# Making a modulation vector in 48 parts beside the first layer's attention instead of beside its gated heads

## The chip, the cores and the metric

The kernel runs on one core of a Trainium2 chip. The metric is device microseconds of one execution. A core has TensorE (PE in the profile, its weight loads are PEld), VectorE (DVE), ScalarE (ACT), GpSimd (POOL) and SyncE (SP), each with an instruction queue of its own that is worked off in order, and 16 DMA engines that are fed from the queues of SP and, for some loads, of POOL.

## The reference

Two blocks are computed in float32 on a sequence of 1024 tokens of width 1024. The first block has two layers. Layer 0 projects its input to eight heads of banded attention (three dilations, 1, 4 and 16) and to four heads of a gated scan in both directions; their outputs are gated and projected back (`w_out_ab`), and a layer norm follows. Layer 1 has twelve gated-scan heads. The second block is a modulated mixer (pooling, state-space and delta-rule branches) and a mixture of 16 experts.

What the change touches is one small piece of the second block, which depends on nothing that the first computes:

```python
sc = jax.nn.silu(c)
scc = jax.nn.silu(c_ctx)[None]
m_lat = jnp.split(sc @ ada_w[l] + ada_b[l], 6, axis=-1)
m_ctx = jnp.split(scc @ ada_w[l] + ada_b[l], 6, axis=-1)
h_lat = modulate(rms_norm(x, norm1_g[l]), m_lat[0], m_lat[1])
h_ctx = modulate(rms_norm(ctx, norm1_g[l]), m_ctx[0], m_ctx[1])
```

`ada_w` is 1024 x 6144. All 6144 columns are wanted for `sc`, and the first 2048 for `scc`.

## The kernel before, in words

The program is written in tile form: Python code issues instructions in program order, and a scheduler then orders each engine's queue from a plan of its own, in which what stands earlier in the program goes first and later work fills in where an engine is free (a block marked `high_priority` goes ahead of its place). The order of each queue is fixed when the program is built; at run time an engine waits at the head of its queue until what the instruction needs is there.

The order of the program is: `Layer0` is set up; `l0.heads(range(4), early)` runs the four gated heads of layer 0 (`Gated`), each with its projections (matmuls into the PSUM tag `mm`, three for each product, since every operand is split in a high and a low part `whi`/`wlo`, `xh`/`xl`); after head 3, `early` adds the first two input projections of the attention (`l0.inputs`) and, in the kernel before, `modulation()`. Then `l0.attention` runs four pairs of attention heads (`attention_pair`). For each pair there are three dilations `p`, two halves and two steps `tp`, so 4 x 3 x 2 x 2 = 48 steps. A step makes scores on PE (`a`), soft maxes them on DVE and ACT (`p`, `pe`), transposes them on PE through the two one-buffer PSUM tags `tr` and `f`, used in turn by `bank()`, copies them out (`pT`) and multiplies by the values into `o`. `filler` adds the input projections of the later pairs, and the output projection (`OutProj`, matmuls `mm<-whi,yin`) follows in the program and fills in. Its `yin` loads are issued from POOL's queue.

`ada` makes the modulation vector `mods` in 48 blocks of 128 columns. For each block it loads two halves of the weight (`aw`, 128 x 4 x 128, two buffers), multiplies each of the eight 128 x 128 slices by a column of `silu(c)` and adds them up in `aacc`. This is done for the latent vector (v = 0) in all blocks and for the context vector (v = 1) in blocks 0 to 15. A sum is made either on DVE (eight instructions, L961 and L963, each a multiply and add) or on POOL (eight multiplies L966, two double-width adds L967, three adds L969 and L972, in place in `aw`). A matmul with a column of ones (L978) then sums over the partitions into the PSUM tag `f`, DVE adds the bias row `ar` (L979), and the row goes to `mods` in memory (L980). The first readers of `mods` are the rows `msh` and `msc` of the context inputs, which come after the output projection of layer 0. In the kernel before, v = 1 is made on DVE, and v = 0 on DVE in 16 of the 48 blocks (`j % 3 == 2`).

L116 makes `wlo` on POOL. In `Gated.unit`, L187 to L210 are DVE work, L239 and L241 POOL work, L214 and L249 PE work; L288 and L289 (`s_rs`) on POOL come ahead of `s_y` on DVE and the transposes L314. L533 to L537 close an attention pair on DVE.

Of the kernel before, what the change touches and what calls it, by code (L numbers as in the profile page):

```python
# [27 lines left out]
def dap(ap, dims, off=0):  # L28

    return bass.AP(tensor=ap.tensor, offset=ap.offset + off, ap=[list(d) for d in dims])  # L30
# [292 lines left out]
    nc.sync.dma_start(ydram[chunk].rearrange("i p t -> p i t")[:, :, t0:t0 + n], hl.bitcast(F32))  # L323


def attention_pair(g, pool, ydram, pair, qT, qp, kT, gate, vd, bias, spread, before):

# [49 lines left out]
    for p, half in ((0, 0), (0, 1), (1, 0), (1, 1), (2, 0), (2, 1)):  # L379
        o = g.psum("o")  # L380
        if half == 0:
# [4 lines left out]
            if p == 2:  # L386
                v16 = pool.tile([64, 16, P], F32, name="v16", tag="v16", bufs=1)
                nc.sync.dma_start(v16, dap(vd, [[16 * W, 64], [W, 16], [1, P]], f0))
        for tp in range(2):

            Ss = [g.psum("a") for _ in range(2)]
            pts = [pool.tile([P, 512], F32, name="pT", tag="pT", bufs=4) for _ in range(2)]
# [202 lines left out]
def bias_tiles(g, pool, rd, pair):  # L595
    out = []
    for h in range(2):
        ts = []
        for p in range(3):
            n, w = (P, 256) if p < 2 else (64, 64)  # L600
            b = pool.tile([P, w], F32, name=f"bias{h}{p}", tag=f"bias{h}{p}", bufs=1)
            for e in range(P // n):
                g.nc.sync.dma_start(b[n * e:n * e + n],
                                    dap(rd, [[383, n], [1, w]], ((pair * 2 + h) * 3 + p) * P * 384 + 127 + (0 if p < 2 else 64)))
            ts.append(b)
        out.append(ts)
    return out
# [20 lines left out]
class Layer0:  # L628
# [130 lines left out]
                self.head(h, gp, qp)  # L759
                after(h)  # L760

    def attention(self, filler):
        g = self.g
        with g.pool("attn") as ap, g.pool("attn2") as qp:
            self.side, rest = ap, lambda: None
            spread = ap.tile([48, 8, P], F32R, name="spread")
            g.nc.vector.memset(spread.bitcast(F32), 0.0)
            for i in (0, 32):
                g.nc.vector.tensor_copy(spread[i:i + 16].rearrange("r j (h f) -> r j h f", h=2),
                                        g.ident[:16, :16].rearrange("r (h j) -> r j h", h=2)[:, :, :, None].to_broadcast([16, 8, 2, 64]))  # L770
            qp_ = ap.tile([P, T], F32, name="qp")
            for pair in range(4):
                ts = []
                for nm in "qkg":
                    ts.append(qp.tile([P, T], F32, name=nm, tag=nm, bufs=1 + (nm != "g")))
                    g.nc.sync.dma_start(ts[-1], self.store[nm, pair])
                rest = attention_pair(g, ap, self.ydram, pair, ts[0], qp_, *ts[1:], self.vd, bias_tiles(g, ap, self.bd, pair), spread, rest)
                if pair == 3:
                    rest()
                filler(pair)  # L780


class OutProj:
# [155 lines left out]
def ada(g, pool, out):  # L939

    nc, I = g.nc, g.I
    c = pool.tile([P, 2, 8], F32, name="ac")
    sg = pool.tile([P, 2, 8], F32, name="acs")
    nc.sync.dma_start(c, I["c2"])
    sigmoid(g, sg, c)
    nc.vector.tensor_mul(c, c, sg)
    ones = pool.tile([P, 1], F32, name="aones")
    nc.vector.memset(ones, 1.0)
    n = 128
    for j in range(6144 // n):  # L950
        both = j < 2048 // n
        acc = [pool.tile([P, n], F32, name=f"aacc{v}", tag=f"aacc{v}", bufs=1) for v in range(1 + both)]
        for kh in range(2):
            w = pool.tile([P, 4, n], F32, name="aw", tag="aw", bufs=2)
            nc.sync.dma_start(w, I["ada_w"][:, 4 * kh:4 * kh + 4, j * n:(j + 1) * n])
            for v in ((1, 0) if both else (0,)):
                at = lambda k: c[:, v, 4 * kh + k:4 * kh + k + 1]
                if v == 1 or j % 3 == 2:
                    for k in range(4):
                        if kh + k == 0:  # L960
                            nc.vector.tensor_scalar(acc[v], w[:, k], at(k), None, op0=ALU.mult)  # L961
                        else:
                            nc.vector.scalar_tensor_tensor(acc[v], w[:, k], at(k), acc[v], op0=ALU.mult, op1=ALU.add)  # L963
                    continue
                for k in range(4):
                    nc.gpsimd.tensor_scalar(w[:, k], w[:, k], at(k), 0.0, op0=ALU.mult, op1=ALU.add)  # L966
                nc.gpsimd.tensor_add(w[:, 0:2], w[:, 0:2], w[:, 2:4])  # L967
                if kh == 0:
                    nc.gpsimd.tensor_add(acc[v], w[:, 0], w[:, 1])  # L969
                else:  # L970
                    for k in range(2):
                        nc.gpsimd.tensor_add(acc[v], acc[v], w[:, k])  # L972
        for v in range(1 + both):
            r = pool.tile([1, n], F32, name="ar", tag="ar", bufs=1)
            nc.sync.dma_start(r, dap(I["ada_b"], [[0, 1], [1, n]], j * n))
            ps = g.psum("tr")
            with g.tc.high_priority():
                nc.tensor.matmul(ps[:1, :n], ones, acc[v], start=True, stop=True)  # L978
                nc.vector.tensor_add(r, ps[:1, :n], r)  # L979
            nc.sync.dma_start(dap(out, [[0, 1], [1, n]], v * 6144 + j * n), r)  # L980


def rms_rstd(g, pool, xt, n=D, eps=EPS2, junk=None):
# [1265 lines left out]
def body(g, out):  # L2249
# [28 lines left out]
    pe = ExitStack()  # L2278
    pe.enter_context(g.psum_pool("ps1", mm=2, a=2, o=2, tr=1, f=1))
    g.open_w()  # L2280
    def modulation():
        g.aside = "f"
        with g.pool("ada") as ap:
            ada(g, ap, mods)
        g.aside = None
    x0s, l0s, es = ExitStack(), ExitStack(), ExitStack()
    xp = x0s.enter_context(g.pool("x0", "right"))
    l0 = Layer0(g, l0s, load_xT(g, xp, I["xT"]), yd)
# [1 line left out]
    def early(h):  # L2290
        if h == 3:
            l0.inputs(0)
            l0.inputs(1)
            modulation()
    l0.heads(range(4), early)
    ga = gains("gla_gain", 8)
    with es:
        def filler(pair):
            if pair < 2:
                l0.inputs(2 + pair)  # L2300
        l0s.close()
        l0.attention(filler)
        x0s.close()
        out0 = OutProj(g, es, "z0", "right", I["x"], yd, I["w_out0"],
                       lambda c: None if c < 4 else ga[:, c - 4:c - 3])
        for cs in ((4, 5), (6, 7), (8, 9), (1, 2), (10, 11, 0)):
            out0.group(*cs)
        x1s = ExitStack()
        xp = x1s.enter_context(g.pool("x1"))
        xt = [xp.tile([P, 8, T], F32R, name=n) for n in ("x1h", "x1l")]  # L2310
        g.aside = "f"
        with g.pool("cm") as mp:
            cx = context_inputs(g, mp, mods)
        g.aside = None
        states = (g.dram.tile([2, P, 384], F32, name="sstates"), g.dram.tile([3, 2, P, 64], F32, name="gstates"))
        rest = context_path(g, cx, states, "left")

        def aside(parts):
            g.aside = "f"
            for _ in range(parts):  # L2320
                next(rest, None)
            g.aside = None
        aside(4)
        closing(0, out0, "right", x1d, (3,), (), lambda zp, zt, tok: to_feature_major(g, zt, tok, xt))
# [152 lines left out]
```

## Time and profile before

| what | value |
|---|---|
| median of 3 runs | 3604.42 us (3601.4 to 3604.8) |
| the profiled execution | 3603.5 us, span 3601.4 us |
| PE busy | 3217.0 us (89% of the span) |
| DVE busy | 2527.6 us (70%) |
| ACT busy | 1577.9 us (44%) |
| POOL busy | 1383.2 us (38%) |

"Busy" is a sum over the whole span; it says nothing of a stage. A busy PE is not a PE at its peak, since matmuls overlap and their ends are modelled. The granted clock of PE is given as a share of 2.4 GHz; its two levels are 2.4 and 1.2 GHz.

### The profile page before, as it was taken

Reading aid. Unit: us, or ns where it says so; the run is one execution under the profiler, and the core shown is the slowest. Engines: PE = TensorE matmul, PEld = TensorE weight load, DVE = VectorE, ACT = ScalarE, POOL = GpSimd, SP = SyncE. Lnnn points to the kernel's source line nnn. Section 1 sums busy time; section 2 is a strip of 40 time slices with the busy share of each in tenths; the row PEclk is TensorE's granted clock in tenths of the full one; section 3 lists DMA queues with packets and bytes.
Section 4 is the critical chain, followed back from the end, with each engine's and each line's share of the span. In section 5 each row is a group of like instructions: output and inputs, shape, how many; then the busy total and the mean of one; then the engine's idle time right before and its main releaser. Section 6 shows DMA issues by size and latency. Waiting matters only on the chain.

```text
span 3601.4 us, 63422 instructions
## 1 busy us (share of the span) xinstructions
PE 3217.0 (89%) x23688; PEld 2585.4 (72%) x23688; DVE 2527.6 (70%) x5574; ACT 1577.9 (44%) x3344; POOL 1383.2 (38%) x1415
## 2 busy tenths in 40 slices
PE   7998898999979999999999989869897777849997
PEld 6887786766658878788887877656676666637765
DVE  4777664346685686987668677758996665578876
ACT  3444333544424454545546452235342432126765
POOL 4657673000043233433324331443222564335533
PEclk9999999999999999999999999879998888969999
DMA  5233344252343222111112234234345755668994
GB/s 183 77 92 92 95 130 144 80 190 75 100 140 99 64 68 58 55 60 52 41 49 68 66 134 136 82 88 120 103 131 142 168 148 173 230 193 317 378 348 156
DMA packets 374000, 461.27 MB, mean 128 GB/s; under 512 B 150419, under 2 KB 280723, under 8 KB 373692
## 3 DMA queue, kind: packets, MB, share of 16 engines
q1 hardware_dynamic: 359852, 407.93, 36.3%
q0 software_dynamic: 13840, 49.29, 4.4%
q8 instruction: 187, 3.06, 0.4%
q14 instruction: 121, 0.99, 0.1%
HBM read 357.57 MB, written 104.27 MB: 128 GB/s over the span
## 4 chain that ended last, share of the span: by engine, by line
PE 49%; DVE 22%; DMA 9%; issue 8%; POOL 7%; ACT 3%; SPq 2%; DVEq 0%; POOLq 0%; ACTq 0%
PE mm L139 10%; PE mm L140 9%; PE mm L141 9%; POOL aw L966 2%; PE a L249 2%; DVE cacc L1145 2%; PE a L406 1%; PE a L2041 1%; DMA aw<-in_ada_w_dram 1%; DMA srow<-rdsl 1%; PE a L141 1%; PE a L140 1%; PE o L225 1%; PE a L139 1%; POOL wlo L116 1%
## 5 line engine op out<-in xcount | busy, mean ns | idle before, releaser
L116 POOL TENSOR_TENSOR wlo<-wraw,whi 128x1024 fp32r<-128x1024 f32 (+1 forms) x131 | 328.3, 2510 | 525.6 <-ACT whi L115 513.2
L139 PE MATMUL mm<-x1h,whi 128*128 128x512 f32 x576 | 234.9, 408 | 3.3 <-DVE G L921 1.7
L140 PE MATMUL mm<-x1l,whi 128*128 128x512 f32 x576 | 233.4, 405 | 1.7 <-DVE x1l L133 1.7
L141 PE MATMUL mm<-x1h,wlo 128*128 128x512 f32 x576 | 233.5, 405 | 0.0
L139 PE MATMUL mm<-whi,x1h 128*128 128x256 f32 x768 | 221.8, 289 | 0.4 <-DVE G L921 0.4
L141 PE MATMUL mm<-whi,x1l 128*128 128x256 f32 x768 | 219.6, 286 | 0.0
L140 PE MATMUL mm<-wlo,x1h 128*128 128x256 f32 x768 | 219.0, 286 | 0.0
L2029 DVE TENSOR_TENSOR elo<-eraw,ehi 128x1024 fp32r<-128x1024 f32 x136 | 184.8, 1381 | 47.1 <-ACT ehi L2027 46.7
L2027 ACT CAST ehi<-eraw 128x1024 fp32r<-128x1024 f32 x160 | 165.5, 1051 | 99.6 <-PE a L141 35.9
L115 ACT CAST whi<-wraw 128x1024 fp32r<-128x1024 f32 (+1 forms) x131 | 136.1, 1040 | 153.9 <-PE mm L140 76.2
L140 PE MATMUL mm<-wlo,xh 128*128 128x256 f32 x640 | 184.2, 288 | 1.9 <-POOL wlo L116 1.9
L141 PE MATMUL mm<-whi,xl 128*128 128x256 f32 x640 | 184.4, 289 | 0.0
L139 PE MATMUL mm<-whi,xh 128*128 128x256 f32 x640 | 183.6, 288 | 0.9 <-DVE G L623 0.9
L139 PE MATMUL mm<-x2h,whi 128*128 128x512 f32 x400 | 166.9, 417 | 10.2 <-ACT cu L1134 5.6
L139 PE MATMUL mm<-whi,yin 128*128 128x512 f32 x352 | 151.4, 433 | 25.0 <-DVE z L824 14.0
L141 PE MATMUL mm<-x2h,wlo 128*128 128x512 f32 x400 | 164.3, 412 | 0.8 <-POOL wlo L116 0.8
L140 PE MATMUL mm<-x2l,whi 128*128 128x512 f32 x400 | 164.6, 411 | 0.0
L139 PE MATMUL mm<-xh,whi 128*128 128x512 f32 x336 | 138.6, 412 | 20.4 <-ACT whi L115 17.6
L966 POOL TENSOR_SCALAR aw<-aw,ac 128x128 f32<-128x128 f32 x256 | 123.7, 498 | 85.7 <-DMA aw<-in_ada_w_dram 41.6
L139 PEld LDWEIGHTS mm<-whi,x1h 128*128 128x128 f32 x768 | 146.7, 191 | 3.1 <-issue 1.0
L140 PEld LDWEIGHTS mm<-wlo,x1h 128*128 128x128 f32 x768 | 146.7, 191 | 0.6
L141 PEld LDWEIGHTS mm<-whi,x1l 128*128 128x128 f32 x768 | 146.8, 191 | 0.3
(747 smaller groups left out, 10317.0 us busy)
## 6 DMA issues: line engine op xcount, KB each, us to landing
eraw<-in_we_gate_dram SPq DMA_DIRECT2D x64, 512.0 KB
eraw<-in_we_up_dram SPq DMA_DIRECT2D x64, 512.0 KB
eraw<-in_we_down_dram SPq DMA_DIRECT2D x64, 512.0 KB
yin<-yd POOLq DMA_DIRECT2D x29, 1024.0 KB, 9.6
aw<-in_ada_w_dram SPq DMA_DIRECT2D x96, 256.0 KB
yd<-y_hl SPq DMA_DIRECT2D x80, 256.0 KB
wraw<-in_w_dram SPq DMA_DIRECT2D x25, 512.0 KB
wraw<-in_w_out_dram SPq DMA_DIRECT2D x24, 512.0 KB
```

The source lines that it names most:

```text
L115: nc.scalar.copy(hi[:, :sz], raw[:, :sz])
L116: nc.gpsimd.tensor_tensor(lo[:, :sz], raw[:, :sz], hi[:, :sz].bitcast(F32), op=ALU.subtract)
L139: nc.tensor.matmul(ps, sh, mh, start=first and i == 0, stop=False)
L140: nc.tensor.matmul(ps, sh, ml, start=False, stop=False)
L141: nc.tensor.matmul(ps, sl, mh, start=False, stop=last and i == n - 1)
L225: nc.tensor.matmul(up[:, :Vd], kdT[:, i * P:(i + 1) * P], V[:, gi, :], start=True, stop=True)
L249: nc.tensor.matmul(ap[32 * c:32 * c + 32, o + lo:o + hi], sta[:, o + 32 * c:o + 32 * c + 32], mov[:, o + lo:o + hi], start=True, stop=True)
L406: nc.tensor.matmul(Ss[h][:, i * 256:i * 256 + w], q[hs[h], qc:qc + P], k[hs[h], lo:lo + w], start=True, stop=True)
L966: nc.gpsimd.tensor_scalar(w[:, k], w[:, k], at(k), 0.0, op0=ALU.mult, op1=ALU.add)
L1145: nc.vector.scalar_tensor_tensor(acc, u[:, i:i + n], cw[:, i:i + 1], acc, op0=ALU.mult, op1=ALU.add)
L2027: nc.scalar.copy(hi, raw)
L2029: nc.vector.tensor_sub(lo, raw, hi.bitcast(F32))
```

## The change

`ada` becomes a generator that yields after each block, and `modulation()` is gone. `attention_pair` draws the next block at the head of each of its 48 steps, so that each block stands in the program just ahead of a step; the tiles come from the pool `attn2` of the attention. The scratch row `aacc` of v = 0 has two buffers and not one. The work is shared out anew: v = 1 stays on DVE (blocks 0 to 15), v = 0 is made on DVE only in six blocks (`j % 6 == 5` from block 16 on: 17, 23, 29, 35, 41, 47) and on POOL in 42. The matmul and the bias add are no longer marked `high_priority`. The PSUM tag is `f` in both kernels (in the one before by `g.aside`).

```diff
--- before.py
+++ after.py
@@ -323,7 +323,7 @@
     nc.sync.dma_start(ydram[chunk].rearrange("i p t -> p i t")[:, :, t0:t0 + n], hl.bitcast(F32))
 
 
-def attention_pair(g, pool, ydram, pair, qT, qp, kT, gate, vd, bias, spread, before):
+def attention_pair(g, pool, ydram, pair, qT, qp, kT, gate, vd, bias, spread, before, aside):
 
 
 
@@ -387,6 +387,7 @@
                 v16 = pool.tile([64, 16, P], F32, name="v16", tag="v16", bufs=1)
                 nc.sync.dma_start(v16, dap(vd, [[16 * W, 64], [W, 16], [1, P]], f0))
         for tp in range(2):
+            next(aside, None)
 
             Ss = [g.psum("a") for _ in range(2)]
             pts = [pool.tile([P, 512], F32, name="pT", tag="pT", bufs=4) for _ in range(2)]
@@ -759,10 +760,11 @@
                 self.head(h, gp, qp)
                 after(h)
 
-    def attention(self, filler):
+    def attention(self, filler, aside):
         g = self.g
         with g.pool("attn") as ap, g.pool("attn2") as qp:
             self.side, rest = ap, lambda: None
+            aside = aside(qp)
             spread = ap.tile([48, 8, P], F32R, name="spread")
             g.nc.vector.memset(spread.bitcast(F32), 0.0)
             for i in (0, 32):
@@ -774,10 +776,12 @@
                 for nm in "qkg":
                     ts.append(qp.tile([P, T], F32, name=nm, tag=nm, bufs=1 + (nm != "g")))
                     g.nc.sync.dma_start(ts[-1], self.store[nm, pair])
-                rest = attention_pair(g, ap, self.ydram, pair, ts[0], qp_, *ts[1:], self.vd, bias_tiles(g, ap, self.bd, pair), spread, rest)
+                rest = attention_pair(g, ap, self.ydram, pair, ts[0], qp_, *ts[1:], self.vd, bias_tiles(g, ap, self.bd, pair), spread, rest, aside)
                 if pair == 3:
                     rest()
                 filler(pair)
+            for _ in aside:
+                pass
 
 
 class OutProj:
@@ -949,35 +953,38 @@
     n = 128
     for j in range(6144 // n):
         both = j < 2048 // n
-        acc = [pool.tile([P, n], F32, name=f"aacc{v}", tag=f"aacc{v}", bufs=1) for v in range(1 + both)]
+        acc = [pool.tile([P, n], F32, name=f"aacc{v}", tag=f"aacc{v}", bufs=2 - v) for v in range(1 + both)]
         for kh in range(2):
             w = pool.tile([P, 4, n], F32, name="aw", tag="aw", bufs=2)
             nc.sync.dma_start(w, I["ada_w"][:, 4 * kh:4 * kh + 4, j * n:(j + 1) * n])
-            for v in ((1, 0) if both else (0,)):
-                at = lambda k: c[:, v, 4 * kh + k:4 * kh + k + 1]
-                if v == 1 or j % 3 == 2:
-                    for k in range(4):
-                        if kh + k == 0:
-                            nc.vector.tensor_scalar(acc[v], w[:, k], at(k), None, op0=ALU.mult)
-                        else:
-                            nc.vector.scalar_tensor_tensor(acc[v], w[:, k], at(k), acc[v], op0=ALU.mult, op1=ALU.add)
-                    continue
+            at = lambda v, k: c[:, v, 4 * kh + k:4 * kh + k + 1]
+            on_dve = [1] if both else [0] if j % 6 == 5 else []
+            for v in on_dve:
+                a = acc[v]
                 for k in range(4):
-                    nc.gpsimd.tensor_scalar(w[:, k], w[:, k], at(k), 0.0, op0=ALU.mult, op1=ALU.add)
-                nc.gpsimd.tensor_add(w[:, 0:2], w[:, 0:2], w[:, 2:4])
-                if kh == 0:
-                    nc.gpsimd.tensor_add(acc[v], w[:, 0], w[:, 1])
-                else:
-                    for k in range(2):
-                        nc.gpsimd.tensor_add(acc[v], acc[v], w[:, k])
+                    if kh + k == 0:
+                        nc.vector.tensor_scalar(a, w[:, k], at(v, k), None, op0=ALU.mult)
+                    else:
+                        nc.vector.scalar_tensor_tensor(a, w[:, k], at(v, k), a, op0=ALU.mult, op1=ALU.add)
+            if 0 in on_dve:
+                continue
+            a = acc[0]
+            for k in range(4):
+                nc.gpsimd.tensor_scalar(w[:, k], w[:, k], at(0, k), 0.0, op0=ALU.mult, op1=ALU.add)
+            nc.gpsimd.tensor_add(w[:, 0:2], w[:, 0:2], w[:, 2:4])
+            if kh == 0:
+                nc.gpsimd.tensor_add(a, w[:, 0], w[:, 1])
+            else:
+                for k in range(2):
+                    nc.gpsimd.tensor_add(a, a, w[:, k])
         for v in range(1 + both):
             r = pool.tile([1, n], F32, name="ar", tag="ar", bufs=1)
             nc.sync.dma_start(r, dap(I["ada_b"], [[0, 1], [1, n]], j * n))
-            ps = g.psum("tr")
-            with g.tc.high_priority():
-                nc.tensor.matmul(ps[:1, :n], ones, acc[v], start=True, stop=True)
-                nc.vector.tensor_add(r, ps[:1, :n], r)
+            ps = g.psum("f")
+            nc.tensor.matmul(ps[:1, :n], ones, acc[v], start=True, stop=True)
+            nc.vector.tensor_add(r, ps[:1, :n], r)
             nc.sync.dma_start(dap(out, [[0, 1], [1, n]], v * 6144 + j * n), r)
+        yield
 
 
 def rms_rstd(g, pool, xt, n=D, eps=EPS2, junk=None):
@@ -2278,11 +2285,6 @@
     pe = ExitStack()
     pe.enter_context(g.psum_pool("ps1", mm=2, a=2, o=2, tr=1, f=1))
     g.open_w()
-    def modulation():
-        g.aside = "f"
-        with g.pool("ada") as ap:
-            ada(g, ap, mods)
-        g.aside = None
     x0s, l0s, es = ExitStack(), ExitStack(), ExitStack()
     xp = x0s.enter_context(g.pool("x0", "right"))
     l0 = Layer0(g, l0s, load_xT(g, xp, I["xT"]), yd)
@@ -2291,7 +2293,6 @@
         if h == 3:
             l0.inputs(0)
             l0.inputs(1)
-            modulation()
     l0.heads(range(4), early)
     ga = gains("gla_gain", 8)
     with es:
@@ -2299,7 +2300,7 @@
             if pair < 2:
                 l0.inputs(2 + pair)
         l0s.close()
-        l0.attention(filler)
+        l0.attention(filler, lambda ap: ada(g, ap, mods))
         x0s.close()
         out0 = OutProj(g, es, "z0", "right", I["x"], yd, I["w_out0"],
                        lambda c: None if c < 4 else ga[:, c - 4:c - 3])
```

## Rows read from the trace of the kernel before

**Rows 1.** The page: busy tenths of an engine in 40 slices of the span.

```profile
PE   7998898999979999999999989869897777849997
...
POOL 4657673000043233433324331443222564335533
```

**Rows 2.** Busy time by stage: stretch, length, engines in the heading's order, clock, DMA.

```profile
core 0: us, PE busy (x) PEld busy (x) DVE busy (x) ACT busy (x) POOL busy (x), PEclk, DMA share, GB/s
20.00:60.00 40.00, 36.15 (x138) 25.93 (x137) 17.58 (x37) 11.91 (x19) 25.77 (x33) 0.91 0.65 193
60.00:280.00 220.00, 218.84 (x1798) 192.03 (x1798) 159.85 (x440) 86.32 (x188) 125.11 (x177) 1.00 0.30 89
280.00:480.00 200.00, 172.80 (x1350) 143.57 (x1349) 133.36 (x352) 81.06 (x198) 147.88 (x232) 0.94 0.32 96
480.00:600.00 120.00, 115.44 (x809) 94.99 (x807) 74.06 (x186) 43.23 (x100) 74.72 (x108) 1.00 0.39 123
...
625.00:815.00 190.00, 183.39 (x1280) 132.80 (x1279) 78.78 (x294) 98.46 (x287) 13.09 (x9) 0.96 0.43 135
815.00:1018.00 203.00, 197.17 (x1252) 138.98 (x1249) 137.59 (x356) 82.48 (x248) 14.16 (x13) 0.98 0.29 91
1120.00:2120.00 1000.00, 965.06 (x8387) 824.08 (x8386) 737.03 (x2078) 509.95 (x1277) 350.70 (x365) 0.99 0.19 58
```

**Rows 3.** The same view for instructions on `aw` alone: DVE and POOL busy.

```profile
60.00:280.00 220.00, 69.30 (x160) 66.75 (x133) 1.00 0.30 89
280.00:480.00 200.00, 18.59 (x48) 98.34 (x180) 0.94 0.32 96
...
sum 580.00, DVE 107.80 POOL 220.21; mean DVE 26.95 POOL 55.05
```

**Rows 4.** Who PE waited for, 280 to 480 us: total, times, longest.

```profile
PE a L214 <- DVE u_kd L210: 6.9, 4, 2.9
PE tr L314 <- DVE s_y L291: 4.1, 2, 2.6
PE a L249 <- POOL u_qh L239: 3.8, 4, 2.6
PE f L978 <- POOL aacc L972: 3.7, 4, 1.4
```

**Rows 5.** Instructions on tile `aw`: duration ns min/median/max, first and last start.

```profile
L966 POOL TENSOR_SCALAR aw<-aw,ac x256: 363/374/2561, 21.1 to 562.9; 128x128 f32<-128x128 f32 x128
L963 DVE SCALAR_TENSOR_TENSOR aacc<-aw,ac,aacc x224: 313/352/2389, 21.0 to 573.3; 128x128 f32<-128x128 f32 x112
L955 SPq DMA_DIRECT2D aw<-in_ada_w_dram x96: 367/379/932, 10.8 to 566.8; - x96
L967 POOL TENSOR_TENSOR aw<-aw x64: 718/738/1269, 23.1 to 564.0; 128x256 f32<-128x256 f32 x64
L972 POOL TENSOR_TENSOR aacc<-aacc,aw x64: 447/461/727, 27.3 to 566.3; 128x128 f32<-128x128 f32 x64
```

**Rows 6.** The chain that ended last, 62 to 67 us: start, duration, link.

```profile
62.10 0.24 PE mm L141
...
66.44 0.31 PE f L978 x2
66.75 0.32 PE mm L141
```

**Rows 7.** Who PE waited for in the attention, 612 to 1018 us, longest first.

```profile
PE o L480 <- DMA v<-vd: 5.6, 2, 5.0
```

**Rows 8.** Instructions on tile `ar`, with durations as in rows 5.

```profile
L979 DVE TENSOR_TENSOR ar<-f,ar x64: 253/272/280, 31.6 to 580.5; 1x128 f32<-1x128 f32 x64
L980 SPq DMA_DIRECT2D mods<-ar x64: 215/243/354, 31.9 to 580.8; - x64
```

**Rows 9.** Instructions in order of time near 575 us: start, duration, engine, what.

```profile
574.82 2.69 POOL L116 TENSOR_TENSOR wlo<-wraw,whi 128x1024 fp32r<-128x1024 f32 x1 [6.44 <-ACT whi L115]
...
575.59 2.21 DVE L187 TENSOR_TENSOR u_kb<-u_b 128x256 f32<-128x256 f32 x1
```

**Rows 10.** DVE groups in the attention, 600 to 1018 us: busy, mean ns.

```profile
L536 DVE TENSOR_TENSOR osb<-osb 128x512 f32<-128x512 f32 x16 | 17.2, 1075 | 0.1
```

## The prediction

> **What bounds the kernel now.** I read the slices of the page first. PE is at eight or nine tenths in nearly every slice of the first third, so PE's queue sets the end of these stages, and only time in which PE stands still or runs at the lower clock can be won there. POOL's line has a hole: after the seventh slice come four zeros, the attention [rows 1]. That is where the change puts the work.
>
> Then the stages, with three numbers of each: PE's gap (length less busy), its clock, POOL's busy share [rows 2]. The gated heads of layer 0 fall in three parts. From 60 to 280 us PE's gap is 1.2 us of 220 at full clock, though the modulation is running: its instructions hold DVE for 69.30 us and POOL for 66.75 us there [rows 3]. From 280 to 480 us PE's gap is 27.2 us of 200 and the mean clock 0.94, and POOL is 74% busy, 98.34 us of it the modulation's. From 480 to 600 us the gap is 4.6 us of 120. Together 32.9 us of 540. In the attention (625 to 1018 us) the gap is 12.4 us of 393, and POOL is busy for only 27.3 us. The gated heads of layer 1, with none of this work beside them (1120 to 2120 us), are the measure of what is ordinary: 34.9 us of 1000, or 3.5%.
>
> Last, what ended PE's waits in the bad stretch [rows 4]. One is the modulation itself (L978 for `aacc`, 3.7 us). Two stand behind POOL's queue, which the modulation fills: L249 for `u_qh` (3.8 us), and L314 for `s_y`, which needs `s_rs` of POOL (4.1 us). The largest, L214 for `u_kd` (6.9 us), is late on DVE, which the modulation also loads.
>
> **The change part by part.** *Heads, waits taken away.* If the heads then look like the ordinary gated stage, their gap falls from 32.9 to 0.035 x 540 = 18.9 us: 14 us won. If they all look like 60 to 280 us (0.5%), it falls to 2.9 us: 30 us won. I take 22, since the four wait rows come to 18.5 us and at least three of them pass through POOL's queue. *Clock.* A mean of 0.94 over 200 us is 12 us of full clock missing, and at PE's busy share of 86% about 10 us of work. The ordinary stage stands at 0.99, so some stays; I take 8, bounds 5 and 10. *Start.* From 20 to 60 us PE's gap is 3.9 us while POOL does modulation; I take 1, bounds 0 and 3. Sum for the heads: 31 us won, between 19 and 43.
>
> *PE's own share of the modulation.* The pair of matmuls L978 takes 0.31 us of the chain, and the next matmul 0.32 instead of 0.24 us [rows 6]: 0.39 us, 64 times, 25 us. It leaves one stage where PE is full and enters another. In the attention its neighbours are plain float32 too and may not pay the 0.08, so 20 to 25 us are added; I take 22, a net gain of 3.
>
> *POOL in the attention.* A block costs 8 x 0.374 + 2 x 0.738 + 3 x 0.461 = 5.85 us at the medians [rows 5] (L969 taken like L972); as loaded in the heads it was 220.21 / 32 = 6.9 us [rows 3]. 42 blocks are 246 to 289 us, and with the 27.3 us already there POOL is 66 to 76% busy of some 416 us. That lies between the good stretch (57%) and the bad one (74%), nearer the bad one. But in the attention nothing else of PE hangs on POOL except `wlo` and the `yin` loads, so the row to scale is L978's: 3.7 us over 180 POOL instructions [rows 3, 4], some 14 blocks of 13, or 0.27 us each; times 42 it is 11 us. Since a block has 416 / 48 = 8.7 us if they come evenly, I take 8; bounds 0 and 15.
>
> *The bank `f`.* Each L978 holds it until DVE's add, 0.31 + 0.27 us [rows 6, 8], 64 times, 37 us in all, in which the attention's transposes have only `tr`. No row shows this use. Nothing excludes 0, since PE has projection matmuls in hand between; the upper bound I set at 12, a third of the holds. I take 4.
>
> *SP's queue.* 96 loads of 0.379 us and 128 small transfers of 0.243 us (loads of `ar` taken like its stores) are 67.5 us of issuing [rows 5, 8], moved in front of the attention's loads of values, weights and bias. A store of `mods` must wait for DVE's add, and what is behind it waits too. PE waits 5.6 us for `v` in this stage today [rows 7]; doubling that is the upper bound, 6; I take 3. In the heads the same queue is freed, which I count at nothing: no PE wait there is on a load.
>
> *DVE.* 22 sums of eight instructions at 0.352 us and 64 adds at 0.272 us are 79 us [rows 5, 8]; DVE goes from 216.4 to 295 us of 393 before the stage is lengthened, 55 to 75%. Two thirds of it falls on blocks 0 to 15, in the first third of the attention, where DVE is only 41% busy [rows 2]. I take 2, bounds 0 and 8. DVE's modulation work leaves the heads (107.80 us, rows 3), which is already in the 22.
>
> *The readers of `mods`* come after the attention; the last block stands ahead of its last step, and POOL's total fits, so I count nothing; if it were late, the context inputs would wait by as much as the last block is late.
>
> Sum: -31 - 3 + 8 + 4 + 3 + 2 = -17 us. Against the profiled execution, 3603.5 us (2.1 us of it outside the span), this gives 3586.5, say 3587. That execution lies 0.9 us under the median of the runs, 3604.42.
>
> **The Trainium skill against this.** Where POOL's `wlo` runs 2.69 us, a DVE instruction of 128 x 256 that starts inside it takes 2.21 us and ends with it [rows 9]. The Trainium skill (SBUF — State Buffer, section "SBUF: two separate sides") gives a reason: DVE with two SBUF inputs and GpSimd share one port pair as an exclusive lock, held for a whole instruction. The trace agrees here, 2.21 us beside 2.69. By that rule the attention's own two-input DVE work would now meet POOL all the time; what this would do is the third rival below.
>
> **The rivals.** *First, slower: POOL paces PE.* PE's queue has the 64 L978 in a fixed place. If these places ask for a block more often than every 6.9 us, each one stalls PE and every matmul behind it, in the way of 280 to 480 us. Over some 300 us of modulation, 13.6% of gap is 41 us, and 6% of clock at 86% busy is 15 us. In place of the 8 us this gives 3587 + 48 = 3635. For it: the share of 76%. Against it: 8.7 us a block if they are spread.
>
> *Second, no change:* the waits of 280 to 480 us are the ordinary ones of gated heads, bunched. Then the heads give 14 + 5 us and the net 3 goes to nothing, while the attention pays its 17: 3603.5 - 2 = 3601. For it: L214 for `u_kd` is the largest row and is not on POOL. Against it: 60 to 280 us.
>
> *Third, DVE in the attention is held up by POOL.* The sixteen `osb` additions of 1.075 us [rows 10] and the 176 instructions of the sums would each wait up to one POOL instruction, 0.738 us [rows 5], half of it on the mean: 192 x 0.37 = 71 us more on DVE, 75 to 93% busy, by which the attention becomes DVE's in its first third. I price it at a third of these 71, 24 us: 3611. Against it: most of the DVE work of this stage reads PSUM.
>
> *Fourth, all gained:* the heads give 43 and the attention hides everything but PE's own matmuls in its 12.4 us of gaps: 3603.5 - 43 - 3 = 3558.
>
> **How the numbers follow.** My own forecast has 0.40, the first rival 0.18, the second 0.20, the third 0.08, the fourth 0.14. The predicted time is that of the forecast, 3587; with its own bounds (19 to 43 won, 0 to 41 paid) it reaches from about 3560 to 3610. The range for 8 in 10 goes down to the fourth rival and up to 3626, a little short of the first: 3558 to 3626. A measurement of this kernel tells about 0.2%, 7 us, from no change. Faster by more: 0.36 of the forecast, 0.14 of the fourth, 0.06 of the second, 0.56. Slower by more: 0.17 of the first, 0.05 of the third, 0.05 of the second and of the forecast's edge, 0.27. Within: 0.17.
>
> **What will show it.** In the profile after, the gated heads should end 45 to 65 us earlier (31 of waits and clock, 25 of PE's own), with a PE gap under 4% and no stretch like 280 to 480 us; the attention should last 25 to 50 us longer, POOL near 70% busy in it. I am wrong if the heads keep a stretch with a clock of 0.94, or if PE's waits in the attention name `aacc` with more than 15 us in all, or if DVE's sums there average far above 0.35 us with PE waiting on `pT` or `p`. If the attention grows by over 70 us, the first rival holds.

## The result and the profile after

The kernel after takes 3745.25 us (median of 4 runs, 3742.47 to 3754.13), the one before 3603.89 beside it: a ratio of 1.0398 (95% interval 1.038 to 1.0416), 141 us slower, where 17 us faster was forecast and 3626 was the upper end. The profiled execution is 3754.13 us with a span of 3752.4.

The page of the kernel after, busy tenths and granted clock in 40 slices [rows 1]:

```profile
PE   7999989978897999999999999969898577768997
...
POOL 2333324355645233443333423252321565234433
PEclk9999999965577999999999999979998778878999
```

POOL's hole is filled, and POOL is nowhere over six tenths. What is new is in PEclk: from the ninth slice on the clock stands at five to seven tenths for five slices of 94 us. The stages, as in [rows 2]: the heads, then the first pair of the attention (565 to 789 us), then the other three:

```profile
core 0: us, PE busy (x) PEld busy (x) DVE busy (x) ACT busy (x) POOL busy (x), PEclk, DMA share, GB/s
...
60.00:280.00 220.00, 218.47 (x1903) 201.61 (x1901) 103.46 (x279) 92.94 (x207) 66.80 (x49) 1.00 0.15 48
280.00:480.00 200.00, 190.52 (x1559) 166.39 (x1559) 112.00 (x318) 91.13 (x219) 68.86 (x59) 0.97 0.20 66
...
565.00:789.00 224.00, 206.27 (x1133) 151.43 (x1132) 113.77 (x318) 63.57 (x165) 96.38 (x173) 0.94 0.45 148
789.00:1113.00 324.00, 273.76 (x1467) 176.09 (x1466) 165.18 (x545) 118.77 (x376) 186.13 (x395) 0.63 0.38 111
```

The heads did what was forecast: PE's gap from 280 to 480 us fell from 27.2 to 9.5 us, the clock rose to 0.97. Their last `gm` on DVE (tile `gm`, first and last start) before and after:

```profile
L748 DVE TENSOR_TENSOR gm<-gm,ge x32: 407/426/2193, 40.6 to 574.2; 128x256 f32<-128x256 f32 x32
```

```profile
L749 DVE TENSOR_TENSOR gm<-gm,ge x32: 407/425/2524, 37.4 to 523.2; 128x256 f32<-128x256 f32 x32
```

That is 51.0 us earlier. All of it and much more is lost in the attention, read here from the first soft max (`pe`) to the copy `mlT` that ends a pair: 361.5 us before (623.1 to 984.6), 548.1 after (565.2 to 1113.3), so that its end lies 128.7 us later than before; the other 22 us between the two executions (3603.5 and 3754.1) lie behind it and were not taken apart. Most of the growth is in the first pair. The instructions on tile `mm` alone, that is the projection and output matmuls that fill PE between the steps, in the first pair and in the other three; columns are length, PE busy, clock, DMA share, GB/s. Before:

```profile
623.10:692.90 69.80, 29.99 (x198) 1.00 0.35 99
692.90:984.60 291.70, 144.94 (x535) 0.96 0.38 119
```

After:

```profile
565.20:788.70 223.50, 151.80 (x687) 0.94 0.45 148
788.70:1113.30 324.60, 31.70 (x115) 0.63 0.38 111
```

The first pair grew by 153.7 us and holds 121.8 us more of filling work. The other pairs lost 113 us of it and did not become shorter for that, but 33 us longer, at a clock of 0.63. The counts of the groups tell two kinds of filling apart: of some 400 matmuls of the input projections (`xh`, `xl`) 198 stood in the first pair before, and all 399 stand there after; of the output projection (`yin`) none stood there before, and 288 do after. Waits of the kernel after, 560 to 1115 us (total, times, longest):

```profile
POOL aw L973 <- DVE aacc L966: 129.4, 16, 29.8
...
DVE ar L985 <- PE f L984: 51.5, 29, 6.6
ACT pe L367 <- PE f L434: 49.9, 13, 15.3
...
PE f L434 <- DVE ar L985: 13.8, 8, 5.0
...
PE f L452 <- DVE ar L985: 6.8, 4, 5.5
...
PE f L984 <- POOL aacc L979: 1.9, 2, 1.0
```

PE waits only 1.9 us for a sum of POOL (L979; its weight loads 4.1), and 20.6 us with transposes (L434, L452) for the add of a closing that still holds `f`. For the rest it is the others that wait for PE: DVE 51.5 us for the matmul L984, ACT 49.9 us behind the transposes L434. PE was at something that stands ahead in its queue. The Trainium skill (PSUM — Partial Sum Buffer, section "Engine vs sequencer instructions") says that matmuls start and complete in program order; these rows agree: DVE waits 51.5 us for a matmul for whose sums PE itself hardly waited.

### The profile page after: what moved, and what is told of

It is laid out like the page before. It is cut to its first block, busy times and chain, and to the rows that moved or that the text cites. A ratio compares the mean times of both kernels' runs of the same rounds, so it can differ in the third digit from the quotient of the medians.

```text
span 3752.4 us, 63473 instructions
## 1 busy us (share of the span) xinstructions
PE 3307.6 (88%) x23688; PEld 2650.4 (71%) x23688; DVE 2491.0 (66%) x5494; ACT 1580.1 (42%) x3344; POOL 1451.2 (39%) x1545
## 4 chain that ended last, share of the span: by engine, by line
PE 34%; DVE 16%; issue 6%; DMA 6%; ACT 2%; POOL 2%; SPq 1%; DVEq 0%; POOLq 0%; ACTq 0%
PE mm L139 6%; PE mm L140 6%; PE mm L141 6%; DVE cacc L1152 2%; PE a L249 1%; PE a L2048 1%; PE a L140 1%; PE a L141 1%; PE a L139 1%; DVE elo L2036 1%; PE f L1110 1%; PE o L225 1%; DMA z<-x1d 1%; DMA yin<-yd 1%; DVE u_kd L210 1%
## 5 line engine op out<-in xcount | busy, mean ns | idle before, releaser
L973 POOL TENSOR_SCALAR aw<-aw,ac 128x128 f32<-128x128 f32 x336 | 135.9, 423 | 232.1 <-DVE aacc L966 129.4
L141 PE MATMUL mm<-whi,x1l 128*128 128x256 f32 x768 | 219.9, 287 | 0.0
L239 POOL TENSOR_TENSOR u_qh<-u_qa,facY 128x256 f32<-128x256 f32 x64 | 75.0, 1172 | 288.8 <-DVE u_qa L236 261.7
L239 POOL TENSOR_TENSOR u_qh<-u_qa,facX 128x256 f32<-128x256 f32 x64 | 69.8, 1090 | 268.3 <-DVE u_qa L236 224.5
L367 ACT ACTIVATE pe<-p,ml 128x192 f32<-128x192 f32 (+2 forms) x192 | 81.4, 425 | 202.4 <-PE f L434 49.9
L139 PE MATMUL mm<-xh,whi 128*128 128x512 f32 x336 | 139.2, 414 | 20.8 <-ACT whi L115 17.0
```

What stands on the lines that cost most here:

```text
L139: nc.tensor.matmul(ps, sh, mh, start=first and i == 0, stop=False)
L141: nc.tensor.matmul(ps, sl, mh, start=False, stop=last and i == n - 1)
L239: nc.gpsimd.tensor_tensor(v3(qh, 32), v3(qa, 32), bcast(fqh, nck, 32), op=ALU.mult)
L367: nc.scalar.activation(pe[:, off:off + w], pt[:, :w], AF.Exp, bias=nm, scale=-1.0, accum_out=l)
L973: nc.gpsimd.tensor_scalar(w[:, k], w[:, k], at(0, k), 0.0, op0=ALU.mult, op1=ALU.add)
```

## The experiments

A block has two parts: the sums, and what I call its closing: the bias row `ar`, the matmul L984 into `f`, DVE's add, the store to `mods`. The kernel before was run again beside each set of runs and took 3600 to 3608 us, so totals of different sets compare to some 8 us. The table gives ratio and interval to the kernel before, the length of the first pair and of the other three, and the time of `mm` matmuls in each (all read as above).

| run | us | ratio (95%) | first pair, its `mm` | other pairs, their `mm` |
|---|---|---|---|---|
| before | 3603.89 | 1 | 69.8, 30.0 | 291.7, 144.9 |
| after | 3745.25 | 1.0398 (1.038 to 1.0416) | 223.5, 151.8 | 324.6, 31.7 |
| 1 old place | 3626.61 | 1.0074 (1.0058 to 1.0091) | 69.6, 30.1 | 288.0, 147.2 |
| 2 place alone | 3730.15 | 1.0339 (1.0322 to 1.0357) | 219.9, 156.3 | 331.7, 33.8 |
| 3 rows only | 3541.39 | 0.9839 (0.9822 to 0.9855) | 70.2, 30.6 | 298.4, 147.7 |
| 4 ready sums | 3685.38 | 1.0226 (1.0206 to 1.0247) | 186.9, 133.0 | 301.5, 55.0 |
| 5 ready sums, 4 rows | 3649.40 | 1.014 (1.0121 to 1.0158) | 168.5, 115.0 | 301.7, 73.2 |
| 6 bank alone | 3660.07 | 1.0147 (1.0123 to 1.017) | 156.4, 99.4 | 305.8, 92.5 |
| 7 rows only, one bank | 3672.90 | 1.0205 (1.0188 to 1.0222) | 144.7, 84.7 | 341.9, 116.1 |
| 8 own bank | 3726.86 | 1.0346 (1.0329 to 1.0364) | 155.6, 90.7 | 386.0, 112.3 |
| 9 one step later | 3721.54 | 1.0304 (1.0283 to 1.0326) | 190.5, 132.5 | 345.4, 60.6 |
| 10 from the end | 3746.48 | 1.041 (1.0391 to 1.043) | 134.2, 82.3 | 431.9, 139.2 |
| 11 three `aw` | 3730.68 | 1.0361 (1.0344 to 1.0379) | 224.5, 153.7 | 313.3, 32.7 |
| 12 closed last | 3643.04 | 1.0116 (1.0099 to 1.0133) | 78.1, 33.7 | 317.9, 153.3 |
| 13 closed last, three `aw` | 3617.23 | 1.0039 (1.0028 to 1.0051) | 82.8, 36.4 | 313.7, 152.0 |
| 14 latent rows late | 3588.56 | 0.9944 (0.9928 to 0.9961) | 86.4, 35.9 | 301.8, 146.0 |
| 15 context rows in steps | 3600.11 | 1.0000 (0.9988 to 1.0012) | 83.6, 35.8 | 344.8, 189.5 |

**Which part of the change it is.** 1, old place: modulation beside the heads again, new sharing kept.

```diff
-            next(aside, None)
...
             l0.inputs(1)
+            modulation()
```

> The modulation is put back beside the gated heads, with the new sharing between DVE and POOL (42 sums on POOL, 22 on DVE) and the priority of before. Both theories: within 15 us of before, 3590 to 3620, since neither sees a cause in the sharing. If the sharing itself costs, over 3640.

Measured 3626.61: the attention is as before (69.6 + 288.0 us), so the place is the cause; the heads end at 586.0 us in place of 574.2, so the new sharing costs some 12 us where it stands there; the total is 7 us over the bracket, and what lies behind the heads of that was not taken apart. 2, place alone:

```diff
-            on_dve = [1] if both else [0] if j % 6 == 5 else []
+            on_dve = ([1] if both else []) + ([0] if j % 3 == 2 else [])
...
+            with g.tc.high_priority():
```

> The kernel after with the old sharing between DVE and POOL (v = 0 on DVE in every third block) and with the matmul and the add marked as going ahead again: of the change only the new place is left. If the place sets the time, 3725 to 3755 as after. If the larger share on POOL costs what the first rival said, 48 us less than after: 3690 to 3705.

3730.15. POOL's larger share and the mark cost about 15 us together (21 by the ratios), the place the rest. That POOL paces PE would have shown as 48.

**Sums or closing.** 3, rows only, has neither sums nor weight loads nor the matmul and add; `ar` is loaded and stored.

```diff
...
-            ps = g.psum("f")
-            nc.tensor.matmul(ps[:1, :n], ones, acc[v], start=True, stop=True)
-            nc.vector.tensor_add(r, ps[:1, :n], r)
```

> Sums, weight loads, matmuls and adds of the modulation are left out; only the 64 bias rows pass through in the 48 steps, so the output is that of a modulation without its matrix product. Both theories expect the heads to end some 52 us earlier than before, as in the changed kernel, and the attention to last about as long as before (357 us from first to last soft max); about 3550 us. If it stays over 3600, the loss is in something that neither theory has.

3541.39: with the heads cleared and nothing in the attention but the rows, 62 us are won. Its `mm`, in the first pair and in the others, against which the next runs are read:

```profile
561.20:631.40 70.20, 30.60 (x198) 1.00 0.34 99
631.40:929.80 298.40, 147.65 (x552) 0.94 0.36 117
```

4, ready sums, takes a constant for `acc`, with the whole closing in its place:

```diff
-        acc = [pool.tile([P, n], F32, name=f"aacc{v}", tag=f"aacc{v}", bufs=2 - v) for v in range(1 + both)]
...
+        acc = [zero, zero]
```

> The sums and the loads of the weight are left out (one constant row stands for all of them); the 64 matmuls, bias adds and stores stay in their steps and in the PSUM bank f. Theory of the bank (a block's use of f stands ahead of a step's own uses, so each step waits for the row load, the add and the store of its block, the planned order spends the projection matmuls early, and the rest of the attention runs with PE at its lower clock level): most of the loss stays, 3680 to 3750 us. Theory of the load (POOL, DVE and the weight loads slow the attention): the loss is gone, about 3570 us.

3685.38; `mm` in the first pair and in the others:

```profile
563.70:750.60 186.90, 133.04 (x601) 0.96 0.39 129
750.60:1052.10 301.50, 55.02 (x203) 0.73 0.22 66
```

So 144 of the 204 us between "rows only" and the kernel after come with the closing, though a closing costs PE 0.3 us, and 60 with the sums. 5 gives the row four buffers in addition:

```diff
-            r = pool.tile([1, n], F32, name="ar", tag="ar", bufs=1)
+            r = pool.tile([1, n], F32, name="ar", tag="ar", bufs=4)
```

> Left out, as in the run with ready sums: the weight loads and the sums (the matmul takes a row of zeros). In addition the bias row ar has four buffers, so that a closing (load of ar, matmul in f, add, store of mods) needs nothing of the closing before. Theory A, the bank f hands a step the time of the block's way through sums and row: with neither left, a closing costs PE about 0.6 us, the first pair is back near 75 us and the attention near 370, total 3545 to 3580. Rival B, the queue of PE: the projection matmuls still stand early in it, because the closings stand in the order of the bank; then the first pair lasts 110 to 150 us with PE full at 1.00, the other 36 steps have no cover and stay near 300 us at a clock of 0.6 to 0.7, total 3620 to 3665. With the ready sums and one row it was 3685.

3649.40, in the rival's bracket, though the first pair is longer than its 110 to 150 us and the later clock, 0.77, higher than its 0.6 to 0.7. Here a transpose waits at most 0.3 us for a closing's add in `f`, and the first pair is still 168.5 us, 115.0 of them `mm`. My theory of that time, that a step lasts as long as its block's way through the bank, falls. 6 also takes the row's load and store out of the steps:

```diff
-            nc.sync.dma_start(r, dap(I["ada_b"], [[0, 1], [1, n]], j * n))
...
-            nc.vector.tensor_add(r, ps[:1, :n], r)
-            nc.sync.dma_start(dap(out, [[0, 1], [1, n]], v * 6144 + j * n), r)
+            nc.vector.tensor_add(r, ps[:1, :n], row)
```

> As the run with ready sums and four rows, and in addition no bias row is loaded and no row stored in the steps: a closing is the matmul into f and DVE's add of a made row, nothing else; the rows of mods (one and the same) are stored after the last step. Left out: loads, sums, bias rows. Theory A, the matmul into f in each step's place is what brings the projection matmuls forward in PE's queue: the first pair stays at 130 to 170 us with 90 to 115 us of projection in it, total 3615 to 3650. Rival C, the loads and stores of rows in SP's queue do it: the first pair is back at 70 to 80 us with 30 us of projection, total 3545 to 3565.

3660.07, 10 us over theory A's bracket, with the first pair inside it (the 64 stores now stand in a bunch ahead of the context inputs, which begin at 1089.1 us as in run 5, though the attention ends 8 us earlier): a matmul into `f` and its add, in each step's place, are enough. Not tested is the same matmul in another bank while the transposes keep both of theirs. `mm` in the first pair and in the others, and the only wait of a transpose for a closing's add, run 6:

```profile
562.60:719.00 156.40, 99.37 (x459) 0.96 0.42 134
719.00:1024.80 305.80, 92.47 (x343) 0.81 0.24 74
...
PEld f L452 <- DVE ar L965: 0.3, 1, 0.3
```

**What the matmul in `f` takes away.** 7 is run 3, with no closing at all, but with the transposes in one bank:

```diff
     def bank():
-        turn[0] ^= 1
-        return g.psum(("tr", "f")[turn[0]])
+        return g.psum("tr")
```

> The run without sums, loads and matmuls (3541), with the attention's transposes in the one bank tr in place of tr and f in turn. There is no closing at all. Theory, the want of a second bank: the first pair lasts 105 to 140 us with 75 to 95 us of projection matmuls in it, the other steps stay near 300 us, total 3590 to 3650. Rival, standing behind a closing: the first pair stays near 70 to 80 us and the total at 3541 to 3560.

3672.90, above the bracket: 132 us more than run 3, for nothing but the second bank. Its `mm`:

```profile
562.00:706.70 144.70, 84.65 (x411) 0.92 0.44 143
706.70:1048.60 341.90, 116.05 (x436) 0.79 0.22 68
```

The same picture without any modulation: filling work early, a lower clock later. The waits that grow are those for transposes (560 to 1110 us, the two largest of six rows):

```profile
ACT pe L366 <- PE tr L445: 76.8, 23, 6.6
DVE pT L374 <- PE tr L446: 71.8, 28, 8.5
```

All six rows, ACT's and DVE's for the matmuls of L433, L445, L446 and L451, come to 304 us (175.7 and 128.6); in both banks they come to 106 in run 3 (59.4 and 46.3) and to 115 in the kernel before (61.3 and 53.6).

8 makes the same edit in the kernel after, so that `f` is left to the closings:

> The kernel after, with the transposes in tr alone, so that f is left to the closings; nothing is left out. No transposes wait for a closing any more, but the attention has one bank less. If waiting behind the closings is the larger part of the loss, a bank less makes the kernel faster: the attention falls from 542 to 420 to 480 us, total 3620 to 3690. If the want of a bank is the whole loss, there is nothing to win: 3735 us or more.

3726.86, between the brackets. The first pair falls from 223.5 to 155.6 us, close to run 7, but the other pairs grow to 386.0. A bank for the closings alone gives back in one place what it costs in the other.

**The sums.** 9 draws the closing of a block one step later, with one more buffer for each `aacc` and three for `ar`.

```diff
...
+        late.append((j, acc))
+        if len(late) > 1:
+            close(*late.pop(0))
```

> The kernel after, with the closing of a block (row, matmul in f, add, store) drawn one step later, three buffers of ar and one more of each aacc; nothing is left out. Theory: the sums come one step ahead, so that the part which they added (542 us of attention against 480 with ready sums) goes, but the projection matmuls still stand early: attention 465 to 500 us, total 3650 to 3695. If waiting for the sums is the whole of the loss: total 3595 to 3620. If it is nothing: 3735 to 3750.

3721.54, missed: the first pair is as with ready sums (190.5 beside 186.9 us), but the other pairs grow to 345.4. 10 turns the order of the blocks round:

```diff
-    for j in range(6144 // n):
+    for j in reversed(range(6144 // n)):
```

> The kernel after with the blocks in the order 47 to 0: the sixteen blocks with two sums and two rows fall on the last 16 steps in place of the first 16. If a step lasts as long as its block, the first pair shrinks from 224 us to 12 x 11 = 130 us, and the last 16 steps grow to 15 to 18 us each, from 9: the sum stays within 3715 to 3765. If the doubled blocks are not what makes the first pair long, it stays near 224 us there, and the end does not grow.

3746.48, as expected, and so is the first pair, now with one closing in a step: 134.2 us with 82.3 of `mm`. The last steps grow less than expected: the last eight copies `osb` of half a dilation (two steps each) stand at 933.6 to 1127.6 us, 13.9 us a step, where they took 8.6 after (992.3 to 1113.1). 11 gives `aw` three buffers:

> The kernel after, with three buffers of aw in place of two. If the blocks' pace of 10.7 to 11 us is set by the loads of the two half buffers (POOL waited 76 us for them), the attention shortens by 20 to 60 us: 3685 to 3725. If it is set by the DVE sums and by the rows that wait for the bank, 3735 to 3750.

3730.68: 15 us less, between the two brackets; the loads set the pace only in part.

**Towards a better version.** 12 keeps the sums in the steps and stores them in memory; 16 closings, 512 columns wide, follow the last step.

```diff
-            r = pool.tile([1, n], F32, name="ar", tag="ar", bufs=1)
...
+            nc.sync.dma_start(park[:, v * 6144 + j * n:v * 6144 + (j + 1) * n], acc[v])
```

> All sums and weight loads stay in the 48 steps, but a finished sum is parked in memory, and the matmuls over the partitions (16 wide ones), adds and stores come after the last step; nothing is left out. Theory of the bank: the attention is back at about 360 to 390 us, 3570 to 3610 us in all. Theory of the load: the attention stays over 480 us, 3690 us or more.

3643.04, 33 us over the bracket of the bank. The attention is back (396.0 us beside 368.6 in run 3), but the sums end only at 1067 us, the last closing at 1088, and the readers of `mods` wait. The loads of the context inputs (tile `cxt`, first and last start), run 12 and run 3:

```profile
L1776 SPq DMA_DIRECT2D cxt<-in_ctx_dram x2: 328/330/332, 1096.9 to 1129.2; - x2
```

```profile
L1743 SPq DMA_DIRECT2D cxt<-in_ctx_dram x2: 328/330/333, 979.7 to 995.2; - x2
```

13 is run 12 with three buffers of `aw`:

> The run in which the sums are parked in memory and closed by 16 wide matmuls after the last step, with three buffers of aw; nothing is left out. There the attention ended near 1005 us but the sums only at 1087, and the context inputs waited. If the loads set the pace of the sums, these end 40 to 90 us earlier and all of it comes off: 3555 to 3605, level with the kernel before or below it. If the place of the blocks in the queues of DVE and SP sets the pace, under 15 us: 3630 to 3643.

3617.23, 12 us over the first bracket: the sums end at 981 us, 86 us earlier, but the 16 closings then run one after the other from 999 to 1046 us. 14 closes only the context rows there and the latent rows after the context inputs, which do not read them:

```diff
+    close_sums(g, pool, park, out, (6, 7))
...
             cx = context_inputs(g, mp, mods)
+        with g.pool("cs") as mp:
+            close_sums(g, mp, parked[0], mods, range(6))
```

> The run with parked sums and three buffers of aw (3617), with only the four wide closings of the context rows (v = 1) after the last step; the twelve of the latent rows (v = 0) come after the context inputs, which do not read them. Nothing is left out. There the 16 closings ran one after the other from 999 to 1046 us and the context inputs stood behind them; with four of them the inputs start some 30 to 40 us earlier, and twelve matmuls of 0.6 us stay to be paid: 3575 to 3600, at or below the kernel before. If something else holds the context inputs, 3610 to 3625.

3588.56, as expected, and below both kernels. Its stages, as in [rows 2]: first pair, other pairs, and from there to the load of the context inputs at 1022 us:

```profile
565.00:651.00 86.00, 81.41 (x601) 61.01 (x600) 50.98 (x189) 41.88 (x131) 58.51 (x120) 0.94 0.54 155
651.00:953.00 302.00, 283.23 (x1827) 197.54 (x1826) 204.24 (x595) 136.97 (x408) 217.43 (x429) 0.95 0.63 190
953.00:1022.00 69.00, 57.88 (x227) 40.03 (x225) 50.12 (x79) 9.24 (x11) 23.64 (x30) 0.95 0.41 131
```

The sums are made beside the attention (POOL 58.51 and 217.43 us) but for the last, which end at 975 us; the filling stays as before, the clock at 0.94 and 0.95, and what is left against run 3 is 16 us in the first pair, 3 in the others and 19 in the last stretch, which takes 50 us there (930 to 980). 15 moves its last four context closings into the last four steps:

> The version that stood at 3588.6 (parked sums, three buffers of aw, the latent rows closed after the context inputs), with the four wide closings of the context rows in the last four steps of the attention in place of behind it. Nothing is left out. The context inputs then need not wait for four closings one after the other (994 to 1012 us): 3565 to 3585. If the four closings in f hold the last steps up by what they save: 3585 to 3600.

3600.11, at the edge of the second bracket: with four closings in `f`, 43 us of output matmuls come forward into the attention (189.5 beside 146.0) and it is 40 us longer. These closings also take two buffers of `aw` each; what that adds was not taken apart.

## Why the prediction was wrong, step by step

**The step that failed** is the bank `f`: "No row shows this use. Nothing excludes 0, since PE has projection matmuls in hand between; the upper bound I set at 12 ... I take 4." Two banks in turn are what lets one transpose be copied out while the next is made. With one bank, run 7, the attention takes 486.6 us in place of 368.6: 118 us. A closing without sums and rows, run 6, takes 462.2: 94 us. I priced the time for which the bank is held, 0.58 us at a time. The transposes' waits for that are 20.6 us in the kernel after, more than my 12, but 0.3 us in run 6, where 94 us are lost all the same. What counts is what PE does meanwhile: in its queue, whose order is fixed before the run, the filling matmuls come forward. Of the input projections half stand in the first pair before and in run 3, and all 399 matmuls after and in runs 6, 7 and 10. With the output projection the filling in the whole attention is 175 to 203 us, 221.4 and 225.3 in runs 10 and 15.

"In hand" the projections were; spent in the first pair they are paid there (the excess of the first pair over its 69.8 us and that of its `mm` over 30.0 us go together: 74.9 and 54.7 in run 7, 86.6 and 69.4 in run 6, 117.1 and 103.0 in run 4, 153.7 and 121.8 after). In the other pairs nothing is saved by the absence of filling: runs 4, 5 and 6 have 55 to 92 us of `mm` there in place of 148 and last 301.5 to 305.8 us, against 298.4 in run 3. PE's busy time less `mm`, closings included, is 194 to 213 us there where run 3 has 141, at a clock of 0.73 to 0.81 in place of 0.94. The filling was not free in itself: at a clock of 0.95, 43 us more of it in run 15 go with 43 us more of length (344.8 beside 301.8). That it is the bank, and not just any matmul in that place, which brings the filling forward is argued from the likeness of runs 6 and 7 and not shown.

**The growth by runs.** Length of the attention: 361.5 before; 368.6 with the rows alone (+7); 462.2 with a matmul in `f` (+94); 470.2 with the rows' loads and stores in the closing (+8); 488.4 with one row buffer (+18); 548.1 with loads and sums (+60). Against the terms: SP's queue and the rows, 3 forecast, up to 6, measured about 26 beside the 7 of the rows alone. POOL and DVE together, 8 + 2 forecast, up to 23, measured 60, of which three buffers of `aw` give back 10 and the old sharing nothing in the attention (551.6 us in run 2). The block's price of 5.85 to 6.9 us was POOL's busy time; its way through two half buffers, DVE and then POOL, is longer. It stood in [rows 5], where 48 blocks go from 10.8 to 566.8 us, 11.6 us each; in the kernel after (tile `aw`):

```profile
L973 POOL TENSOR_SCALAR aw<-aw,ac x336: 363/378/1582, 573.9 to 1086.2; 128x128 f32<-128x128 f32 x168
L968 DVE SCALAR_TENSOR_TENSOR aacc<-aw,ac,aacc x154: 329/352/2440, 573.8 to 1099.5; 128x128 f32<-128x128 f32 x154
```

Again 11 us a block ((1099.5 - 573.9) / 48), against 8.1 us that a step of the later pairs had before (291.7 / 36) and 5.8 in the first pair (69.8 / 12), where I had reckoned with an even 8.7. In run 12, where no matmul waits for a sum, the sums of DVE still take 10.3 us a block (572.0 to 1067.3 us), and 8.6 with three buffers in run 13 (569.7 to 981.0). One sum of the prediction is off, without effect on the range: its own bounds give 3603.5 - 19 - 3 + 41, about 3622, and not 3610.

**What was right.** The heads: 31 us of waits and PE's own 25 were to end them 45 to 65 us earlier, measured 51.0, and 62 us in all in run 3. PE's own share in the attention came to 30.5 us and not 22, since L984 takes 329 ns at the mean where L978 took 273. The readers of `mods`, counted at nothing, were indeed not late after, but only because the attention had become so long; in run 12 the loads of the context inputs begin 117 us later than in run 3, 30 us of it by the longer attention, the rest by waiting for `mods`.

**The rivals.** The first, POOL paces PE, gave a slower time but not this mechanism. My sign for it, growth of the attention by over 70 us, came (186.6), and proved a bad sign: most of the loss stays without any sum on POOL (run 4), and PE waited 1.9 us for POOL's sums against my bound of 15. The third, DVE held up by POOL, shows nowhere: the sums of L968 have a median of 352 ns, as those of L963 had [rows 5], and the `osb` additions a mean of 1087 ns beside 1075 [rows 10]. The Trainium skill's rule of an exclusive port (SBUF — State Buffer, section "SBUF: two separate sides") is not refuted by that; its price here is no more than a part of the 60 us. The first rival has the fixed places in PE's queue, but as stalls for a sum; no rival had a bank or filling that comes forward.

**What stays open.** Whether a closing in another bank would cost the same was not tried. Why the other pairs grow in runs 8 and 9 (386.0 and 345.4 us) was not settled, nor how the 60 us divide among loads, DVE and the place of the closings. By which rule the order of PE's queue is made was not tried; that it has the filling matmuls early is read from the counts, and why all of the input projections move into the first pair is not shown. What of the longer steps is the clock and what the missing filling itself was not taken apart.

## What to carry to other kernels

Filling work is limited: before something is put into a loop that lives on it, ask what the addition makes the queue spend, and what the steps that come last will have left. A PSUM bank used in turn is not priced by how long a guest holds it but by what the loop takes without it; a run with one bank less and nothing added came near that price here (118 us of attention beside 94). For the pace of a moved chain take first and last start over its count, not the busy time of one engine.

## What the hardware showed unexpectedly

A low clock with a busy engine: from 789 to 1113 us PE is busy 273.76 of 324 us, yet the granted clock is 0.63 at the mean, so the lower level (1.2 GHz) for most of it, where the same stage of the kernel before had 0.96 with 282.11 of 292 us busy. From 700 to 750 us PE is full at 1.00; then its busy time drops, and the clock falls to the lower level. It rises when PE is full again, near the end of the attention:

```profile
725.00:750.00 25.00, 25.00 (x138) 17.74 (x137) 18.15 (x49) 5.84 (x18) 13.90 (x24) 1.00 0.36 98
750.00:775.00 25.00, 17.68 (x113) 11.86 (x111) 14.99 (x38) 8.92 (x18) 12.96 (x22) 0.85 0.28 85
775.00:800.00 25.00, 16.44 (x67) 8.79 (x67) 14.28 (x51) 5.56 (x20) 13.93 (x27) 0.50 0.21 57
...
1075.00:1100.00 25.00, 25.00 (x192) 17.94 (x189) 14.18 (x52) 6.30 (x29) 11.12 (x26) 1.00 0.29 65
```

In the three pairs the attention's own matmuls, with `mm` and the closings taken off, hold PE for 222 us (274.4 - 31.7 - 20.5) in place of 137 (281.8 - 144.9) for the same work. "Busy" therefore hid the loss: read it together with the clock.
